# Where weight tiles begin within 128 bytes of SBUF in a two-layer decoder trunk

## The chip, the cores and the metric

One core of one Trainium2 chip runs the whole program in one launch. The metric is the device time of that launch in microseconds (us), lower is better. SBUF is the core's working memory: 128 partitions, and a tile is a run of bytes at the same address in every partition. Addresses below are bytes within a partition.

## What is computed

Two layers over 256 tokens of width 1024, all in float32, and a final norm (cut from the reference):

```
for l in range(2):
    hn = rms_norm(h, mix_norm_g[l])
    if l == 0: mix = even_mixer(hn, ...)   # softmax attention (8 heads x 64, rotary)
                                           # beside gated linear attention (8 heads), one output projection
    else:      mix = odd_mixer(hn, ...)    # gate branch x (width-4 conv -> RG-LRU recurrence), output projection
    h = h + mix
    h = h + conv_ffn(rms_norm(h, ffn_norm_g[l]), w_up, conv_w, conv_b, w_down)
return rms_norm(h, final_norm_g)

def conv_ffn(x, w_up, conv_w, conv_b, w_down):     # width 1024 -> 2 x 3072 -> 1024
    h = causal_dwconv(x @ w_up, conv_w, conv_b)    # width-3 depthwise convolution
    u, g = split(h, 2)
    return (u * gelu(g)) @ w_down
```

## The kernel before

Activations are kept with features on partitions and the 256 tokens along the row. All large weights are cut on the host into 204 chunks of 128 partitions x 1024 float32 (512 KB), in the order of use. A chunk is 8 blocks of 128 x 128.

A matmul with full float32 precision is made of three passes. Every operand is split in a high part (rounded to the format fp32r, which TensorE takes in one pass) and the low rest. `issue_w` (L123) fetches chunk i by a DMA of the SP queue into a landing tile `w`, makes the high part `wh` on ScalarE (L134) and the low part `wl` on VectorE (L135). `passes` (L142, matmuls at L146) then issues for each block three matmuls into one PSUM sum: wh times high activation, wh times low activation, wl times high activation. So a chunk makes 24 matmuls of 256 columns, each preceded on TensorE by a load of its 128 x 128 weights, and 204 chunks make 4,896 of them. In the listing of a trace wh, wh, wl follow each other. The split activations are the tiles `x` (input of a stage, L160 `new_x`), `m` and `r` (mixers' outputs) and `y` (FFN, 24 blocks); each of their rows of 256 float32 has 1,024 bytes. In one place, `tok_gemm` (PSUM tile `pst`, 8 chunks of layer 0), the roles are swapped: `x` is the loaded weight and `wh`/`wl` stream through.

The stages in order: layer 0 mixer (PSUM tiles psbq, psbk, psa, pst, psog and the attention pieces; `psout` is the output projection), layer 0 FFN (`psu` up, 96 chunks; `psd` down, 24 chunks), layer 1 mixer (psx, psgb, psgt, psout), layer 1 FFN (psu, psd), final norm. `Norm.rstd` (L181) turns summed squares into the norm's factor: two or four matmuls of one column into `nps` (L187), a square root and a reciprocal on `rtk`, and two transposes of `rtk` into `nps` (L193).

A scheduler fixes the order on each engine when the program is built, and an allocator gives each tile its address then; a tile's buffers are the distinct addresses that it gets. `issue_w` asks for 4 buffers of `w` and 6 of `wh` and `wl` (10 for the ten chunks from 104 on); the allocator may give more where there is room. `load_w` keeps one chunk issued ahead in the program; on the chip ScalarE, VectorE and the DMA queue run ahead as far as buffers allow.

In the built program the tiles that matter begin here (count of tiles by start address modulo 128 bytes):

```
tile                          before                 after
wh (204)                      189 at 96, 15 at 0     204 at 64
wl (204)                      180 at 96, 24 at 0     204 at 64
w, landing (204)              196 at 96, 8 at 0      204 at 0
x (4), m, r, y (FFN, 2)       all at 0               all at 0
chunks with wh and wl at 0    11                     0
chunks with only wl at 0      13                     0
chunks with only wh at 0      4                      0
```

Rows and blocks are multiples of 512 bytes, so every block of a tile has the tile's remainder. The chunks at 0 all lie in layer 1: numbers 106, 107, 124, 141, 147, 153, 159, 165, 171, 177 and 183 (both parts), 119, 123, 142, 148, 154, 160, 166, 172, 178, 184, 196, 197 and 198 (low part only), 118, 132, 186 and 200 (high part only). The landing tile's address comes round after 4 to 7 chunks in layer 0 and after 4 to 27 in layer 1 before (7 at the start of the kernel and in the layer 0 FFN), and after 4 chunks nearly everywhere after the change.

Of the kernel before, what the change touches and what calls it, by code (L numbers as in the profile page):

```python
# [8 lines left out]
F32 = mybir.dt.float32  # L9
F32R = mybir.dt.float32r  # L10
# [12 lines left out]
P = 128  # L23
S = 256
D = 1024
KT = 8
# [3 lines left out]
CW = 1024  # L30
# [18 lines left out]
NV = _o  # L49
# [13 lines left out]
def trunk(ctx: ExitStack, tc: tile.TileContext, xT, w, wgk, wgk2, vec, cst, mskf, out):  # L63
    nc = tc.nc

    cp = ctx.enter_context(tc.tile_pool(name="cp", bufs=1))
    wp = ctx.enter_context(tc.tile_pool(name="wp", bufs=4))
    xp = ctx.enter_context(tc.tile_pool(name="xp", bufs=1))
    tp = ctx.enter_context(tc.tile_pool(name="tp", bufs=2))
    pp = ctx.enter_context(tc.tile_pool(name="pp", bufs=1, space=bass.MemoryType.PSUM))  # L70

    def bank(name, tag="g"):
        return pp.tile([P, 512], F32, tag=tag, bufs=BANKS[tag], name=name)

    def order(first, then):
        tc.add_manual_dep(then.ins, first.ins.name,
                          mybir.DependencyInfo(mybir.DependencyClass.NoSync, mybir.DependencyReason.DATA),
                          reason="issue order")

    big = cp.tile([P, KT * S + P + NV + 8], F32, name="big")  # L80
    h = big[:, 0:KT * S].rearrange("p (k t) -> p k t", k=KT)
    idt = big[:, KT * S:KT * S + P]
    vt = big[:, KT * S + P:KT * S + P + NV]
# [22 lines left out]
    def act(name, *args, **kw):  # L106
        use(name)
        ins = nc.scalar.activation(*args, **kw)
        order(tbl["load"], ins)
        tbl["ops"].append(ins)  # L110
        return ins
# [6 lines left out]
    def load_w():  # L118
        while len(state["q"]) <= LOOK and state["i"] < NCH:
            state["q"].append(issue_w())  # L120
        return state["q"].pop(0)

    def issue_w():  # L123
        i = state["i"]
        state["i"] += 1
        wt = wp.tile([P, CW], F32, tag="w", name=f"w{i}")
        dma = nc.sync.dma_start(wt, w[i])
        if i == 0:
            first.append(dma)
        pre = "p" if L1_C0 <= i < L1_C0 + NPRE else ""  # L130
        nb = NPRE if pre else 6
        wh = wp.tile([P, CW], F32R, tag="wh" + pre, bufs=nb, name=f"wh{i}")
        wl = wp.tile([P, CW], F32R, tag="wl" + pre, bufs=nb, name=f"wl{i}")
        hi = nc.scalar.activation(wh, wt, AF.Copy)  # L134
        lo = nc.vector.tensor_sub(wl, wt, wh.bitcast(F32))  # L135
        for kind, o in (("h", hi), ("l", lo)):
            for before in state["hooks"].pop((kind, i), []):
                order(before, o)
        return wh, wl
# [24 lines left out]
    class Norm:  # L164
# [18 lines left out]
        def rstd(self, copy=True, hook=0):  # L183
            ps = bank("nps", "t")
            for t in range(2):
                for i, s_ in enumerate(self.acc):
                    nc.tensor.matmul(ps[:, t:t + 1], s_[:, t * P:(t + 1) * P], ones, start=i == 0,  # L187
                                     stop=i == len(self.acc) - 1)
            rt = tp.tile([P, 2], F32, tag="rtk", name="rtk")
            root = act(SQRT, rt, ps[:, 0:2], AF.Sqrt, bias=epst, scale=1.0 / D)  # L190
            inv = nc.vector.reciprocal(rt, rt)
            for t in range(2):
                nc.tensor.transpose(ps[:, S + t * P:S + (t + 1) * P], rt[:, t:t + 1].to_broadcast([P, P]), idt)  # L193
            self.tok = rt
            if not copy:
                return ps[:, S:2 * S]
            rs = tp.tile([P, S], F32, tag="rs", name="rs")
            cp_ = nc.scalar.activation(rs, ps[:, S:2 * S], AF.Copy)
            if hook:
                for key, o in zip((("h", hook), ("l", hook), ("h", hook + 1)), (root, inv, cp_)):  # L200
                    state["hooks"].setdefault(key, []).append(o)
            return rs
# [55 lines left out]
    for i in range(4):  # L258
        first.append(nc.sync.dma_start(h[:, 2 * i:2 * i + 2, :], xT[:, 2 * i:2 * i + 2, :]))
    state["q"].append(issue_w())  # L260
    first.append(nc.sync.dma_start(idt, cst[:, 0:P]))
    for a_, b_ in zip(first, first[1:]):
# [16 lines left out]
    with tc.tile_pool(name="l0", bufs=1) as lp, tc.tile_pool(name="l0r", bufs=4) as lr:  # L279
        def nt(name):  # L280
            return lr.tile([P, 512], F32, tag="n", bufs=14, name=name)

        state["q"].append(issue_w())
        state["q"].append(issue_w())
        gk2 = lp.tile([32, 256], F32, name="gk2")
# [82 lines left out]
        lam = vt[:, VOFF["lam"]:VOFF["lam"] + 8]  # L368

        def small(name):  # L370
            return cp.tile([P, 8], F32, name=name)

        e, d2, zz, z2, acc, cc = [small(f"s{i}") for i in range(6)]
        nc.scalar.activation(e, lam, AF.Abs)
        act(LNEXP, e, e, AF.Exp, scale=-1.0)
# [147 lines left out]
            return both  # L523

        def softmax(ps):
            mx = lr.tile([P, 2], F32, tag="mx", name="mx")
            nc.vector.tensor_reduce(mx[:, 0:1], ps[:, 0:128], axis=mybir.AxisListType.X, op=ALU.max)
            nc.vector.tensor_reduce(mx[:, 1:2], ps[:, 128:384], axis=mybir.AxisListType.X, op=ALU.max)
            nc.vector.tensor_scalar(mx, mx, -0.125, None, op0=ALU.mult)
            pe = lr.tile([P, 384], F32, tag="pe", name="pe")  # L530
            sm = lr.tile([P, 2], F32, tag="sm", name="sm")
            act(LNEXP, pe[:, 0:128], ps[:, 0:128], AF.Exp, bias=mx[:, 0:1], scale=0.125, accum_out=sm[:, 0:1])
            act(LNEXP, pe[:, 128:384], ps[:, 128:384], AF.Exp, bias=mx[:, 1:2], scale=0.125, accum_out=sm[:, 1:2])
            nc.vector.reciprocal(sm, sm)
            nc.vector.tensor_scalar(pe[:, 0:128], pe[:, 0:128], sm[:, 0:1], None, op0=ALU.mult)
            nc.vector.tensor_scalar(pe[:, 128:384], pe[:, 128:384], sm[:, 1:2], None, op0=ALU.mult)
            pt = bank("ptr", "t")
            for b in range(3):
                nc.tensor.transpose(pt[:, b * P:(b + 1) * P], pe[:, b * P:(b + 1) * P], idt)
            p_ = lr.tile([P, 384], F32, tag="PT", name="PT", bufs=8)  # L540
            nc.scalar.activation(p_, pt[:, 0:384], AF.Copy)
            return p_
# [3 lines left out]
        for pr in range(4):  # L546
            for j, ps in enumerate(scores(pr)):
                PT[2 * pr + j] = softmax(ps)
            ps = bank("pso", "t")
            for j in range(2):  # L550
                hd = 2 * pr + j
                r = slice(64 * j, 64 * j + 64)
                cs = slice(64 * hd, 64 * hd + 64)
                nc.tensor.matmul(ps[r, 0:S], av[:, 0, cs], PT[hd][:, 0:S], start=True, stop=False)
                nc.tensor.matmul(ps[r, P:S], av[:, 1, cs], PT[hd][:, S:384], start=False, stop=True)
            split(M[:, pr, 0, :], M[:, pr, 1, :], ps[:, :S])
# [26 lines left out]
            gemm(ps[:, :S], load_w(), X)  # L583
            nc.vector.tensor_mul(bog[:, m, :], ps[:, :S], rs)
        act(SILU, bog, bog, AF.Silu)
        rh = lp.tile([P, 16], F32, name="rh")
        act(SQRT, rh, psn[:, 0:16], AF.Sqrt, bias=epst, scale=1.0 / 64)
        nc.vector.reciprocal(rh, rh)
        rb = lp.tile([P, 16, 64], F32, name="rb")
# [268 lines left out]
```

## Time and profile before

| | |
|---|---|
| time, median of 3 runs | 637.37 us (637.22 to 638.85) |
| the profiled execution | 639.27 us, span of its instructions 637.5 us |
| PE (TensorE matmuls) busy | 622.5 us, 98% |
| PEld (weight loads, beside PE) | 608.1 us, 95% |
| DVE (VectorE) busy | 516.8 us, 81% |
| ACT (ScalarE) busy | 402.5 us, 63% |
| DMA | 110.91 MB, mean 174 GB/s |

The span runs from the first to the last instruction; 1.8 us of the profiled execution lie around it. Matmuls overlap each other in the trace: one lasts some 280 ns from its first read to its modelled end, but the next starts some 117 ns after it. So the distance between starts (called the step below) is what a matmul costs, and a busy PE says nothing of it. In a timeline, neighbouring instructions of one kind are merged: `x2` is two of them, and the row's first number is the start of the first.

### The profile page before, as it was taken

Reading aid. Unit: us, or ns where it says so; the run is one execution under the profiler, and the core shown is the slowest. Engines: PE = TensorE matmul, PEld = TensorE weight load, DVE = VectorE, ACT = ScalarE, POOL = GpSimd, SP = SyncE. Lnnn points to the kernel's source line nnn. Section 1 sums busy time; section 2 is a strip of 40 time slices with the busy share of each in tenths; the row PEclk is TensorE's granted clock in tenths of the full one; section 3 lists DMA queues with packets and bytes.
Section 4 is the critical chain, followed back from the end, with each engine's and each line's share of the span. In section 5 each row is a group of like instructions: output and inputs, shape, how many; then the busy total and the mean of one; then the engine's idle time right before and its main releaser. Section 6 shows DMA issues by size and latency. Waiting matters only on the chain.

```text
span 637.5 us, 12979 instructions
## 1 busy us (share of the span) xinstructions
PE 622.5 (98%) x5210; PEld 608.1 (95%) x5210; DVE 516.8 (81%) x899; ACT 402.5 (63%) x654; POOL 33.3 (5%) x58
## 2 busy tenths in 40 slices
PE   7989999999999999999999999999999999999995
PEld 3989988999999999999999999989999999999995
DVE  5799984677999999987688859996999999976532
ACT  7696565766666666665477488865676666674310
POOL 7480000000000000000000000000000000000000
PEclk9999999999999999999999999999999999999998
DMA  8624624324472585555568305554356465455201
GB/s 302 259 97 164 208 92 166 134 103 162 165 284 95 186 294 186 184 196 183 187 226 305 126 2 198 200 190 174 133 200 235 162 229 188 178 212 187 100 1 67
DMA packets 31517, 110.91 MB, mean 174 GB/s; under 512 B 3648, under 2 KB 4192, under 8 KB 31456
## 3 DMA queue, kind: packets, MB, share of 16 engines
q1 hardware_dynamic: 31456, 110.07, 48.4%
q8 instruction: 41, 0.67, 0.4%
q14 instruction: 20, 0.16, 0.1%
HBM read 109.01 MB, written 1.05 MB: 173 GB/s over the span
## 4 chain that ended last, share of the span: by engine, by line
PE 92%; DVE 3%; ACT 2%; issue 1%; DMA 1%; SPq 0%; DVEq 0%
PE psu L146 42%; PE psd L146 21%; PE psout L146 5%; PE pst L146 4%; PE psx L146 4%; PE psgb L146 3%; PE psa L146 2%; PE psog L146 2%; PE psgt L146 2%; DVE wl L135 1%; PE psbq L146 1%; PE pl L462 1%; PE psbk L146 1%; ACT wh L134 1%; DMA big<-xT 1%
## 5 line engine op out<-in xcount | busy, mean ns | idle before, releaser
L134 ACT ACTIVATE wh<-w 128x1024 fp32r<-128x1024 f32 x204 | 212.7, 1057 | 116.3 <-PE psu L146 71.8
L135 DVE TENSOR_TENSOR wl<-w,wh 128x1024 fp32r<-128x1024 f32 x204 | 248.3, 1226 | 41.0 <-ACT wh L134 39.9
L146 PE MATMUL psu<-x,wh 128*128 128x256 f32 x1536 | 270.5, 280 | 0.0
L146 PEld LDWEIGHTS psu<-x,wh 128*128 128x128 f32 x1536 | 234.4, 188 | 0.0
L146 PE MATMUL psu<-x,wl 128*128 128x256 f32 x768 | 214.1, 279 | 0.0
L146 PEld LDWEIGHTS psu<-x,wl 128*128 128x128 f32 x768 | 144.5, 188 | 0.0
L146 PE MATMUL psd<-y,wh 128*128 128x256 f32 x768 | 134.6, 279 | 0.0
L146 PEld LDWEIGHTS psd<-y,wh 128*128 128x128 f32 x768 | 117.0, 188 | 0.0
L146 PE MATMUL psd<-y,wl 128*128 128x256 f32 x384 | 106.6, 279 | 0.0
L644 DVE SCALAR_TENSOR_TENSOR c<-v,big,c 128x255 f32<-128x255 f32 (+1 forms) x192 | 84.4, 484 | 0.0
L146 PEld LDWEIGHTS psd<-y,wl 128*128 128x128 f32 x384 | 72.1, 188 | 0.0
L642 ACT ACTIVATE c<-v,big 128x256 f32<-128x256 f32 x96 | 51.7, 588 | 0.5 <-DVE v L637 0.5
L172 ACT ACTIVATE sq<-big 128x256 f32<-128x256 f32 x40 | 15.4, 407 | 50.8 <-DVE big L211 50.8
L211 DVE TENSOR_TENSOR big<-big,psd 128x256 f32<-128x256 f32 x16 | 6.7, 420 | 35.1 <-PE psd L146 35.1
L637 DVE TENSOR_TENSOR v<-psu,rs 128x512 f32<-128x512 f32 x48 | 33.0, 690 | 0.0
L146 PE MATMUL psout<-r,wh 128*128 128x256 f32 x128 | 23.1, 281 | 2.0 <-DVE r L729 2.0
L146 PE MATMUL pst<-wh,x 128*128 128x256 f32 x128 | 24.6, 288 | 0.0
L146 PE MATMUL psa<-x,wh 128*128 128x256 f32 x128 | 22.7, 280 | 1.8 <-DVE kn L394 1.8
L146 PE MATMUL psout<-m,wh 128*128 128x256 f32 x128 | 23.6, 286 | 0.0
L146 PE MATMUL psx<-x,wh 128*128 128x256 f32 x128 | 23.0, 281 | 0.0
L146 PE MATMUL psgb<-x,wh 128*128 128x256 f32 x128 | 22.7, 280 | 0.0
L99 ACT ACT_TABLE_LOAD x17 | 21.8, 1283 | 1.0 <-PEq L850 0.7
(200 smaller groups left out, 862.2 us busy)
## 6 DMA issues: line engine op xcount, KB each, us to landing
w<-w SPq DMA_DIRECT2D x204, 512.0 KB, 4.2
big<-xT SPq DMA_DIRECT2D x4, 256.0 KB, 4.9
out<-o SPq DMA_DIRECT2D x4, 256.0 KB, 2.4
ct<-cst SPq DMA_DIRECT2D x1, 384.0 KB, 7.6
big<-vec SPq DMA_DIRECT2D x1, 224.0 KB, 8.1
mf<-mskf SPq DMA_DIRECT2D x1, 192.0 KB, 5.0
wg<-wgk SPq DMA_DIRECT2D x1, 64.0 KB, 2.1
big<-cst SPq DMA_DIRECT2D x1, 64.0 KB, 7.2
```

Of the source, the lines that this page charges most:

```text
L99: ld = nc.scalar.preload_act_table_set(name)
L134: hi = nc.scalar.activation(wh, wt, AF.Copy)
L135: lo = nc.vector.tensor_sub(wl, wt, wh.bitcast(F32))
L146: out.append(nc.tensor.matmul(ps, a, b, start=first and i + j == 0, stop=last and i == n - 1 and j == 2, skip_group_check=skip))
L172: ins = nc.scalar.activation(sq, t, AF.Square)
L211: add = nc.vector.tensor_add(h[:, m, :], h[:, m, :], ps)
L462: nc.tensor.matmul(pv[:, :, :, cs], Kb[li, I][:, ts_], qv[:, :, :, cs], start=True, stop=True)
L637: nc.vector.tensor_mul(v, ps.rearrange("p (j t) -> p j t", j=2), rs[:, None, :].to_broadcast([P, 2, S]))
L642: nc.scalar.activation(c[:, j, :], v[:, j, :], AF.Identity, bias=V("fc_b", layer * 48 + ch), scale=wv(2))
L644: nc.vector.scalar_tensor_tensor(c[:, j, d:], v[:, j, 0:S - d], wv(2 - d), c[:, j, d:], op0=ALU.mult, op1=ALU.add)
```

## The change

The allocator packs tiles tightly, at multiples of 32 bytes. Tiles whose length is no multiple of 128 bytes are made longer until it is (`big`, `rtk`, the small tiles `s0` to `s5`, `mx`, `sm`, `rh`); `w`, `wh` and `wl` get 128 bytes more, and the used 4,096 bytes of `wh` and `wl` begin 64 bytes into them. What is computed stays as it was.

```diff
-    big = cp.tile([P, KT * S + P + NV + 8], F32, name="big")
+    big = cp.tile([P, -(-(KT * S + P + NV + 8) // 32) * 32], F32, name="big")
...
-        wt = wp.tile([P, CW], F32, tag="w", name=f"w{i}")
+        wt = wp.tile([P, CW + 32], F32, tag="w", name=f"w{i}")[:, 0:CW]
         dma = nc.sync.dma_start(wt, w[i])
...
-        wh = wp.tile([P, CW], F32R, tag="wh" + pre, bufs=nb, name=f"wh{i}")
-        wl = wp.tile([P, CW], F32R, tag="wl" + pre, bufs=nb, name=f"wl{i}")
+        oh, ol = 16, 16
+        wh = wp.tile([P, CW + 32], F32R, tag="wh" + pre, bufs=nb, name=f"wh{i}")[:, oh:oh + CW]
+        wl = wp.tile([P, CW + 32], F32R, tag="wl" + pre, bufs=nb, name=f"wl{i}")[:, ol:ol + CW]
...
-            rt = tp.tile([P, 2], F32, tag="rtk", name="rtk")
+            rt = tp.tile([P, 32], F32, tag="rtk", name="rtk")[:, 0:2]
...
-            mx = lr.tile([P, 2], F32, tag="mx", name="mx")
+            mx = lr.tile([P, 32], F32, tag="mx", name="mx")[:, 0:2]
```

The built program has the same instructions with other addresses, and lines from L132 on have moved by one. The order changes in the layer 0 mixer alone, in few places; the largest shift is around the first norm. On PE, in the second chunk of psbq and the first of psbk, before:

```order
L146 MATMUL psbq<-x,wh_158 128x256 x2
L146 MATMUL psbq<-x,wl_159 128x256
L146 MATMUL psbq<-x,wh_158 128x256 x2
L146 MATMUL psbq<-x,wl_159 128x256
L146 MATMUL psbk<-x,wl_165 128x256
L146 MATMUL psbk<-x,wh_164 128x256
L187 MATMUL nps<-big,ssq 128x1 x2
L146 MATMUL psbk<-x,wh_164 128x256
```

and after:

```order
L147 MATMUL psbq<-x,wl_159 128x256
L188 MATMUL nps<-big,ssq 128x1 x2
L147 MATMUL psbq<-x,wh_158 128x256 x2
L147 MATMUL psbq<-x,wl_159 128x256
L147 MATMUL psbq<-x,wh_158 128x256 x2
L147 MATMUL psbq<-x,wl_159 128x256
L147 MATMUL psbk<-x,wl_165 128x256
L147 MATMUL psbk<-x,wh_164 128x256 x2
```

The norm's sums now follow 44 of the chunk matmuls instead of 52, and its two transposes 73 instead of 87; the next step that needs the norm on PE, `psz` (L348), follows 96 in both. On VectorE, the conversions and the norm's sums of the same stretch, before:

```order
L135 TENSOR_TENSOR wl_165<-w_162,wh_164 128x1024
L179 TENSOR_TENSOR ssq<-ssq,sq 128x256
L135 TENSOR_TENSOR wl_373<-w_370,wh_372 128x1024
L179 TENSOR_TENSOR ssq<-ssq,sq 128x256
L135 TENSOR_TENSOR wl_403<-w_400,wh_402 128x1024
L135 TENSOR_TENSOR wl_446<-w_443,wh_445 128x1024
L191 RECIPROCAL rtk<-rtk 128x2
```

and after:

```order
L136 TENSOR_TENSOR wl_165<-w_162,wh_164 128x1024
L180 TENSOR_TENSOR ssq<-ssq,sq 128x256 x2
L136 TENSOR_TENSOR wl_373<-w_370,wh_372 128x1024
L136 TENSOR_TENSOR wl_403<-w_400,wh_402 128x1024
L192 RECIPROCAL rtk<-rtk 128x2
L136 TENSOR_TENSOR wl_446<-w_443,wh_445 128x1024
```

The last sum of squares and the reciprocal each moved ahead of one conversion. The SP and POOL queues keep their order.

## Rows read from the trace of the kernel before

**Rows 1.** The page: busy time of the engines, and the chain of work that ended last by engine.

```profile
PE 622.5 (98%) x5210; PEld 608.1 (95%) x5210; DVE 516.8 (81%) x899; ACT 402.5 (63%) x654; POOL 33.3 (5%) x58
...
PE 92%; DVE 3%; ACT 2%; issue 1%; DMA 1%; SPq 0%; DVEq 0%
```

**Rows 2.** What PE waited for over the whole span: us in total, times, longest.

```profile
PE psout L146 <- DVE r L729: 2.0, 2, 1.5
PE psa L146 <- DVE kn L394: 1.8, 1, 1.8
...
PE psbq L146 <- ACT wh L134: 0.9, 1, 0.9
...
PE psbq L146 <- DVE wl L135: 0.8, 1, 0.8
```

**Rows 3.** Busy time by stretch (layer 0 FFN up and down, layer 1 FFN up and down): us, PE busy (x instructions), PEld, DVE, ACT, POOL, granted clock, DMA share, GB/s.

```profile
155.00:275.00 120.00, 120.00 (x1031) 120.00 (x1030) 114.96 (x198) 81.42 (x133) 0.00 (x0) 1.00 0.55 196
275.00:343.00 68.00, 68.00 (x585) 68.00 (x585) 52.35 (x90) 41.27 (x56) 0.00 (x0) 1.00 0.58 205
...
440.00:560.00 120.00, 120.00 (x1023) 120.00 (x1022) 113.41 (x197) 80.50 (x131) 0.00 (x0) 1.00 0.54 193
560.00:628.00 68.00, 68.00 (x583) 68.00 (x582) 34.97 (x55) 26.08 (x36) 0.00 (x0) 1.00 0.31 109
```

**Rows 4.** Timeline of PE in the layer 0 FFN, wh and wl at 96: eight groups of wh, wh, wl lie between the first row and the last.

```profile
199.80 0.40 PE L146 MATMUL psu<-x,wh 128*128 128x256 f32 x2
200.03 0.28 PE L146 MATMUL psu<-x,wl 128*128 128x256 f32 x1
200.15 0.39 PE L146 MATMUL psu<-x,wh 128*128 128x256 f32 x2
...
202.60 0.40 PE L146 MATMUL psu<-x,wh 128*128 128x256 f32 x2
```

**Rows 5.** Timeline of PE in the layer 1 FFN: the first row begins chunk 153 (wh and wl at 0), the row at 487.57 chunk 154 (wl at 0), the last row chunk 155. Four groups of three lie between 486.01 and 487.45.

```profile
484.69 0.40 PE L146 MATMUL psu<-x,wh 128*128 128x256 f32 x2
...
486.01 0.28 PE L146 MATMUL psu<-x,wl 128*128 128x256 f32 x1
...
487.45 0.28 PE L146 MATMUL psu<-x,wl 128*128 128x256 f32 x1
487.57 0.40 PE L146 MATMUL psu<-x,wh 128*128 128x256 f32 x2
...
490.42 0.28 PE L146 MATMUL psu<-x,wh 128*128 128x256 f32 x1
```

**Rows 6.** Timeline of PE in `tok_gemm` of layer 0 (x at 0 loaded, wh and wl at 96 streaming): eleven groups of three lie between the first row and the last.

```profile
54.01 0.40 PE L146 MATMUL pst<-wh,x 128*128 128x256 f32 x2
...
57.91 0.40 PE L146 MATMUL pst<-wh,x 128*128 128x256 f32 x2
```

**Rows 7.** Groups of weight loads in two stretches, 479.1 to 481.7 (wh and wl at 96) and 484.7 to 487.4 (at 0): count, busy us, mean ns of one, idle before.

```profile
L146 PEld LDWEIGHTS psu<-x,wh 128*128 128x128 f32 x16 | 2.4, 188 | 0.0
...
L146 PEld LDWEIGHTS psu<-x,wh 128*128 128x128 f32 x16 | 2.5, 191 | 0.0
```

**Rows 8.** Timeline of the weight loads at the end, where the matmuls between them have one column.

```profile
629.58 0.30 PEld L187 LDWEIGHTS nps<-big,sq 128*128 128x128 f32 x2 [0.93 <-ACT sq L172]
629.80 0.30 PEld L187 LDWEIGHTS nps<-big,ssq 128*128 128x128 f32 x2
630.02 0.30 PEld L187 LDWEIGHTS nps<-big,sq 128*128 128x128 f32 x2
```

**Rows 9.** Timeline of the first 41 us, PE and then DVE: the norm's sums and transposes, psz, and the wait for `kn`.

```profile
20.16 0.50 PE L187 MATMUL nps<-big,ssq 128*128 128x1 f32 x4
...
24.69 0.38 PE L193 MATMUL nps<-big,rtk 128*128 128x128 f32 x2
...
26.28 1.13 PE L348 MATMUL psz<-bgk,gk 32*128 32x256 f32 x4
...
40.56 0.48 PE L146 MATMUL psa<-x,wh 128*128 128x256 f32 x2 [1.76 <-DVE kn L394]
...
16.51 1.31 DVE L135 TENSOR_TENSOR wl<-w,wh 128x1024 fp32r<-128x1024 f32 x1
17.74 0.72 DVE L179 TENSOR_TENSOR ssq<-ssq,sq 128x256 f32<-128x256 f32 x1
...
31.42 1.44 DVE L135 TENSOR_TENSOR wl<-w,wh 128x1024 fp32r<-128x1024 f32 x1 [0.34 <-ACT wh L134]
32.79 1.13 DVE L357 SCALAR_TENSOR_TENSOR G<-z,az 128x512 f32<-128x512 f32 x1
34.02 4.52 DVE L362 TENSOR_TENSOR_SCAN cum<-cum,G 128x512 f32<-128x512 f32 x3
38.47 1.35 DVE L135 TENSOR_TENSOR wl<-w,wh 128x1024 fp32r<-128x1024 f32 x1
39.74 0.68 DVE L394 TENSOR_TENSOR kn<-psbk,rs 128x512 f32<-128x512 f32 x1
```

**Rows 10.** The page's groups of the two conversions and its row of the chunk DMA (count, KB each, median us to landing); then from the timelines the low part of chunk 49 (DVE), the high part of chunk 53 (ACT) and the low part of chunk 53 (DVE), counted in the program's order.

```profile
L134 ACT ACTIVATE wh<-w 128x1024 fp32r<-128x1024 f32 x204 | 212.7, 1057 | 116.3 <-PE psu L146 71.8
L135 DVE TENSOR_TENSOR wl<-w,wh 128x1024 fp32r<-128x1024 f32 x204 | 248.3, 1226 | 41.0 <-ACT wh L134 39.9
...
w<-w SPq DMA_DIRECT2D x204, 512.0 KB, 4.2
...
177.62 1.25 DVE L135 TENSOR_TENSOR wl<-w,wh 128x1024 fp32r<-128x1024 f32 x1
...
186.23 1.06 ACT L134 ACTIVATE wh<-w 128x1024 fp32r<-128x1024 f32 x1 [0.45 <-PE psu L146]
...
187.85 1.25 DVE L135 TENSOR_TENSOR wl<-w,wh 128x1024 fp32r<-128x1024 f32 x1
```

More of the change, by code (lines that the diff above doesn't have):

```diff
@@ L370, in small @@
         def small(name):
-            return cp.tile([P, 8], F32, name=name)
+            return cp.tile([P, 32], F32, name=name)[:, 0:8]
         e, d2, zz, z2, acc, cc = [small(f"s{i}") for i in range(6)]
@@ L530, in softmax @@
             pe = lr.tile([P, 384], F32, tag="pe", name="pe")
-            sm = lr.tile([P, 2], F32, tag="sm", name="sm")
+            sm = lr.tile([P, 32], F32, tag="sm", name="sm")[:, 0:2]
             act(LNEXP, pe[:, 0:128], ps[:, 0:128], AF.Exp, bias=mx[:, 0:1], scale=0.125, accum_out=sm[:, 0:1])
@@ L585, in trunk @@
         act(SILU, bog, bog, AF.Silu)
-        rh = lp.tile([P, 16], F32, name="rh")
+        rh = lp.tile([P, 32], F32, name="rh")[:, 0:16]
         act(SQRT, rh, psn[:, 0:16], AF.Sqrt, bias=epst, scale=1.0 / 64)
```

## The prediction

> **What bounds the kernel now.** I read the page first. PE is busy for 98% of the span, and the chain of work that ended last runs through PE for 92% of it [rows 1]. A busy PE alone does not prove a bound, so I read next what PE waited for. The waits are few: 2.0 us for `r`, 1.8 us for `kn`, and under 1 us each for the first chunk's two conversions, the only time that PE waits for `wh` or `wl` at all [rows 2]. So DMA, ScalarE and VectorE deliver in time, and the time is the number of matmuls times the step between them. [...]
>
> The third view is the timeline of PE, for the step. In the layer 0 FFN 24 matmuls take 202.60 - 199.80 = 2.80 us, 116.67 ns each [rows 4]. The reader is to see that this is not the same everywhere. In chunk 153 twelve steps take 487.45 - 486.01 = 1.44 us, 120.0 ns each [rows 5]; the code, the shape and the stage's other work are those of its neighbours, but `wh` and `wl` begin at 0 modulo 128 bytes there and at 96 elsewhere. In `tok_gemm`, with the roles swapped, 33 steps take 57.91 - 54.01 = 3.90 us, 118.2 ns each [rows 6]. So the step depends on where the two operands lie. Taking the loaded operand's remainder minus the streamed one's, modulo 128: at 0 the step is 120.0, at 32 (0 - 96) 118.2, at 96 116.67. The loads show it too: 191 ns each at 0, 188 at 96 [rows 7].
>
> The change puts this difference at 64 in every chunk, `tok_gemm` included (0 - 64 is 64 too). No row shows 64. That is the one unknown that matters: there are 204 x 24 = 4,896 such matmuls, so one nanosecond of step is worth 4.9 us.
>
> **The change part by part.**
>
> *Chunks at 0 go away.* A chunk with both parts at 0 lasts 487.57 - 484.69 = 2.88 us, one with only `wl` at 0 490.42 - 487.57 = 2.85 us [rows 5], against 2.80 us [rows 4]. If the new place costs what 96 costs, the 11 chunks of the first kind give 11 x 0.08 = 0.88 us, the 13 of the second 13 x 0.05 = 0.65 us. The 4 with only `wh` at 0 are not among the rows; I take 0.05 as well, 0.2 us. Sum 1.7 us.
>
> *`tok_gemm`.* 8 x 24 = 192 steps from 118.2 to 116.67 give 0.3 us.
>
> *The other 168 chunks, 4,032 steps, go from 96 to 64.* The bounds from the nearest rows: above, the worst step seen, 120.0 ns, +3.33 x 4,032 = +13.4 us. Below, the loads' own pace: where the matmuls between have one column, a pair of loads starts 0.22 us after the pair before, 110 ns each [rows 8]. That is -6.67 ns a step. But VectorE is busy 114.96 and 113.41 of the 120.00 us of the up-projections [rows 3], which can therefore shrink by 5.0 and 6.6 us at most. The other 2,592 matmuls (4,896 less the 96 chunks of up-projection) would give 17.3 us; together about -29 us.
>
> Between these ends I take no change, 116.67 ns, for this reason. During a step the matmul reads 256 x 4 = 1,024 bytes of a partition and the next load 512. The matmul's reading place gains 512 bytes on the load's, four times 128, in every step, whatever the start; so the start can only decide whether one meeting more falls inside the step. That fits steps that differ by about one unit, 120.0 - 116.67 = 3.33 ns, and a value between for 32, where some steps would have the extra meeting and some not. Then the long steps fill one stretch of differences that holds 0 and ends near 32, and 96 is outside it. 64 lies between 32 and 96, outside as well. This is an inference from three points; a straight line from 32 to 96 would give 117.4 ns at 64, +3.1 us on the 4,032 steps. I count it in the rival below.
>
> *The first norm moves ahead* on PE by 8 matmuls (its sums) and 14 (its transposes), 0.9 and 1.6 us at 117 ns. Its sums start at 20.16 now [rows 9]; 0.9 us earlier the last sum of squares, which now also leads one conversion on VectorE, still stands before it: it ends at 18.46 now and about 1.2 us earlier then. The norm comes 1.6 us sooner, but `psz` keeps its place on PE (26.28), and the wait that follows, 1.76 us for `kn`, hangs on G, the scans and the conversion before `kn` on VectorE. G starts at 32.79, right behind a conversion (31.42, 1.44 us) that waited for its high part, and that one isn't touched. So the wait stays: 0 us, give or take 0.5.
>
> *Landing tiles come round after 4 chunks instead of up to 7.* The DMA of chunk k waits then for the low part of chunk k - 4. In the layer 0 FFN the low part of chunk 49 ends at 178.86 and the high part of 53 begins at 186.23 [rows 10]: 7.4 us, and a landing takes 4.2. The cover is 3.2 us there, and behind it the lead of a finished chunk before its use: chunk 53's low part ends at 189.1, and its matmuls are those of 200.1 on [rows 4, 10], 11 us later. Cost nothing. Without this cover a chunk would cost 4.2 + 1.06 + 1.23 = 6.5 us instead of 2.8.
>
> *Conversions and other tiles* at new addresses: VectorE and ScalarE have idle time in every stage, and nothing waits for them; the padding moves no extra byte. Nothing.
>
> Sum: -1.7 - 0.3 + 0 = -2.0 us. The profiled execution took 639.27 us (637.5 of span), 0.3% over the median; 2.0 us less is 637.3 by its own time, and **635.4 us** by the median of 637.37. A change within 0.3% (1.9 us) can't be told from none for this kernel, so the forecast itself lies on that line.
>
> **The rivals.**
>
> *The step falls further (27%).* 64 is as far from 0 as an address can be. If distance counts, one more unit goes: 113.33 ns, -3.33 x 4,896 = -16.3 us, with the 2.0 us 619.1; half a unit gives 627. For it: the step falls from 0 to 32 and to 96, which is 32 on the other side, and 110 shows room below. Against: 32 and 96, equally far from 0, differ by 1.5 ns, so distance alone isn't the measure. VectorE would still fit, 114.96 in 116.6 us, without room for more.
>
> *The step rises (18%), slower than before.* If 64 belongs to the long stretch with 0 and 32: 118.2 ns is +1.5 x 4,032 = +6.2 us; the chunks at 0 still gain about 0.8 and `tok_gemm` nothing: 643. At 120.0 it is +13.4 us, and +0.3 for each of the two others: 651. It decides from 0.5 ns on, where 4,032 steps eat the 2.0 us. For it: the value at 32 is nearer to 0's than to 96's. It would also come if the pattern repeated every 64 bytes; against that, 32 and 96 would be equal then, and they are not.
>
> *The address plays no part (4%)*, and chunk 153 is slow by what runs beside it: 637.4, no change. Against it stand the same chunks, every sixth one of the layer 1 FFN, and the neighbours at 116.67. [...]
>
> *Fewer landing tiles make PE wait (3%).* Each late chunk costs up to 3.7 us (6.5 - 2.8); two or three where the mixers and FFNs meet make 643 to 647. It decides where the lead of 11 us is gone.
>
> **How the numbers follow.** The forecast has 48%: 635.4, with a range of its own from 634.5 to 637. Its chance falls half on faster by over 0.3% and half within. Faster: 0.24 + 0.27 = 0.51. Same: 0.24 + 0.04 + a hundredth of the rise = 0.29. Slower: 0.17 + 0.03 = 0.20. The range goes from 619, a full unit less, to 645, past the 118.2 ns case; below it lie steps nearer 110 and above it those nearer 120, some 15 in 100 together.
>
> **What would show each step right or wrong.** In the timeline after, 24 matmuls of any FFN chunk in 2.80 us (116.67) with no chunk of 2.85 or 2.88; loads at 188 ns everywhere; 33 steps of `pst` in 3.85 us; 1,031 matmuls in 120 us of the layer 0 up-projection. 2.72 us a chunk is the first rival, 2.84 or more the second. The wait for `kn` near 1.8 us and no wait of PE for `wh` or `wl` past the first chunk show the other terms right. The prediction is wrong above all if 64 isn't like 96: the long stretch of differences may reach further than 32, or the units may not be what they seem.

## The result and the profile after

The changed kernel takes 627.63 us (median of 4 runs, 626.35 to 630.00) against 638.11 us for the kernel before on the same chip: a ratio of 0.984, with an interval of 0.982 to 0.986. That is 10.5 us, 1.6% less, where 2.0 us were forecast. The profiled execution took 628.50 us, its span is 626.7 us; before the span was 637.5 us.

The page and the waits of PE, the rows that answer to [rows 1, 2]:

```profile
PE 609.1 (97%) x5210; PEld 594.1 (95%) x5210; DVE 516.1 (82%) x899; ACT 404.2 (64%) x654; POOL 30.9 (5%) x58
...
PE 87%; DVE 4%; DMA 4%; ACT 3%; issue 2%; SPq 0%; DVEq 0%; ACTq 0%
```

```profile
PE psout L147 <- DVE r L730: 2.6, 2, 1.5
PE psx L147 <- ACT x L206: 2.3, 1, 2.3
PE psa L147 <- DVE kn L395: 1.8, 1, 1.8
```

PE is still the bound, but a wait of 2.3 us for `x` is new, and 4% of the chain now runs through DMA, where it was 1%.

The busy time by stretch of the FFN, as in [rows 3] (us, PE busy with its instructions, PEld, DVE, ACT, POOL, granted clock, DMA share, GB/s), up and down in layer 0, then in layer 1:

```profile
155.00:275.00 120.00, 120.00 (x1061) 120.00 (x1061) 117.63 (x206) 84.46 (x138) 0.00 (x0) 1.00 0.59 202
275.00:340.00 65.00, 65.00 (x576) 64.98 (x574) 46.93 (x80) 37.17 (x47) 0.00 (x0) 1.00 0.65 221
430.00:550.00 120.00, 120.00 (x1061) 120.00 (x1060) 114.51 (x199) 84.24 (x135) 0.00 (x0) 1.00 0.57 198
550.00:620.00 70.00, 68.79 (x607) 68.62 (x605) 37.59 (x59) 28.41 (x40) 0.00 (x0) 1.00 0.37 129
```

A window counts every matmul that lies in it in part, some 2.4 more than begin there: (1,061 - 2.4) x 113.3 ns are the 120 us. Before, 1,031 and 1,023 stood in windows of the same length. VectorE is now busy for 117.63 of 120 us, as close to a bound of its own as the forecast said for this step.

Timeline of PE over the chunk of layer 0 that begins at 197.33 (eight groups of wh, wh, wl between the first row and the last), and over eleven groups of `tok_gemm`:

```profile
197.33 0.39 PE L147 MATMUL psu<-x,wh 128*128 128x256 f32 x2
...
200.05 0.39 PE L147 MATMUL psu<-x,wh 128*128 128x256 f32 x2
```

```profile
51.35 0.40 PE L147 MATMUL pst<-wh,x 128*128 128x256 f32 x2
...
55.23 0.40 PE L147 MATMUL pst<-wh,x 128*128 128x256 f32 x2
```

24 matmuls take 2.72 us, 113.33 ns each, against 116.67 in [rows 4]. In the layer 1 FFN every chunk that nothing interrupts takes 2.72 us too: the chunks of 2.88 and 2.85 us of [rows 5] are gone. In `tok_gemm` the 33 steps of this piece take 3.88 us, 117.6 ns, hardly under the 118.2 of [rows 6]. Over all steps of its 8 chunks that follow each other without a gap the mean is 116.4, and it was 118.4 before.

Where the time went, by stage (us from the first matmul of a stage to the first of the next, read from the starts in the traces; the first line begins with the span, the last ends with the last chunk matmul):

```
stage                       before    after    difference
mixer of layer 0            140.68   139.34      -1.34
FFN of layer 0              202.27   196.71      -5.56
mixer of layer 1             81.98    84.92      +2.94
FFN of layer 1              203.42   196.60      -6.82
```

The two FFNs give 12.4 us. Each has 72 chunks, 48 up and 24 down (the 96 chunks of `psu` named above are those of both layers). The mixers have 1,440 of the 4,896 matmuls, whose steps alone would give 4.8 us at 3.33 ns each; instead the two mixers together are 1.6 us longer. The mixer of layer 1 lost most, and the place to look at is its start. PE, ScalarE and the clock there, after, and ScalarE at the same place before:

```profile
339.79 0.39 PE L147 MATMUL psx<-x,wh 128*128 128x256 f32 x2
342.48 0.39 PE L147 MATMUL psx<-x,wh 128*128 128x256 f32 x1 [2.30 <-ACT x L206]
```

```profile
338.58 1.07 ACT L135 ACTIVATE wh<-w 128x1024 fp32r<-128x1024 f32 x1 [0.34 <-DMA w<-w]
340.66 1.06 ACT L135 ACTIVATE wh<-w 128x1024 fp32r<-128x1024 f32 x1 [1.01 <-DMA w<-w]
341.62 0.40 ACT L173 ACTIVATE sq<-big 128x256 f32<-128x256 f32 x1
341.93 0.49 ACT L206 ACTIVATE x<-big 128x256 fp32r<-128x256 f32 x1
```

```profile
343.80:347.30 3.50, 3.50 (x19) 3.50 (x19) 2.77 (x3) 2.80 (x5) 0.00 (x0) 0.52 0.93 322
```

```profile
342.19 1.06 ACT L134 ACTIVATE wh<-w 128x1024 fp32r<-128x1024 f32 x1 [0.65 <-DMA w<-w]
343.60 0.42 ACT L172 ACTIVATE sq<-big 128x256 f32<-128x256 f32 x1 [0.34 <-DVE big L211]
343.92 0.49 ACT L205 ACTIVATE x<-big 128x256 fp32r<-128x256 f32 x1
```

The last block of `x` (L206) stands on ScalarE behind the high part of chunk 115, and this waits for its DMA. Before, that conversion began at 342.19, 0.8 us ahead of the stage's first matmul (342.94); after, at 340.66, 4.6 us behind it (336.05). So PE waits 2.30 us for `x`, and behind the wait the granted clock is 0.52 in the mean of 3.5 us, with 0.50 from 343.96 to 347.37: 19 matmuls lie in that stretch, which would hold 31 at 113.33 ns, and the steps there are 213 to 218 ns. An estimate of the whole: 2.3 us for `x`, some 1.7 us by the clock (half of the 3.4 us at 0.50), and 0.6 us more of waits for `r`. These 4.6 us are most of the 5.8 that separate +2.94 from what the steps alone would give in this stage (720 x 3.33 ns and 0.4 us for its chunks at 0).

### The profile page after: what moved, and what is told of

Same layout as the page of the kernel before. It is cut to its first block, busy times and chain, and to the rows that moved or that the text cites. A ratio compares the mean times of both kernels' runs of the same rounds, so it can differ in the third digit from the quotient of the medians.

```text
span 626.7 us, 13053 instructions
## 1 busy us (share of the span) xinstructions
PE 609.1 (97%) x5210; PEld 594.1 (95%) x5210; DVE 516.1 (82%) x899; ACT 404.2 (64%) x654; POOL 30.9 (5%) x58
## 4 chain that ended last, share of the span: by engine, by line
PE 87%; DVE 4%; DMA 4%; ACT 3%; issue 2%; SPq 0%; DVEq 0%; ACTq 0%
PE psu L147 42%; PE psd L147 17%; PE psout L147 6%; PE pst L147 4%; PE psgb L147 3%; DMA w<-w 3%; PE psx L147 3%; PE psog L147 2%; DVE wl L136 2%; PE psa L147 2%; PE psgt L147 2%; ACT wh L135 1%; PE psbq L147 1%; PE pl L463 1%; PE pss L520 1%
## 5 line engine op out<-in xcount | busy, mean ns | idle before, releaser
L135 ACT ACTIVATE wh<-w 128x1024 fp32r<-128x1024 f32 x204 | 214.3, 1060 | 141.9 <-PE psu L147 69.5
L136 DVE TENSOR_TENSOR wl<-w,wh 128x1024 fp32r<-128x1024 f32 x204 | 248.2, 1222 | 53.5 <-ACT wh L135 49.3
L147 PE MATMUL psu<-x,wh 128*128 128x256 f32 x1536 | 262.2, 276 | 0.0
L147 PEld LDWEIGHTS psu<-x,wh 128*128 128x128 f32 x1536 | 231.3, 188 | 0.0
L147 PE MATMUL psu<-x,wl 128*128 128x256 f32 x768 | 211.7, 276 | 0.0
L147 PE MATMUL psd<-y,wh 128*128 128x256 f32 x768 | 130.5, 276 | 0.0
L147 PEld LDWEIGHTS psd<-y,wh 128*128 128x128 f32 x768 | 115.5, 188 | 0.0
L147 PEld LDWEIGHTS psx<-x,wh 128*128 128x128 f32 x128 | 20.7, 199 | 2.5 <-ACT x L206 2.5
```

The source lines that it names most:

```text
L147: out.append(nc.tensor.matmul(ps, a, b, start=first and i + j == 0, stop=last and i == n - 1 and j == 2, skip_group_check=skip))
```

## The experiments

Three questions were open: whether the address alone makes the shorter step and by which rule; whether fewer landing tiles cause the wait for `x`; and whether a version without that wait is faster still. All steps below are read from starts in the traces. A table behind the runs puts them beside the addresses.

**Every start from 0 to 120.** One kernel with sixteen starts, eight bytes apart.

```diff
-        oh, ol = 16, 16
+        oh = ol = 2 * (i % 16)
```

> Chunk i has its two split weight tiles at 8 x (i modulo 16) bytes modulo 128 instead of all at 64; the streamed tiles stay at 0 and nothing else differs, so each of the sixteen starts has some six chunks in each up-projection. Known steps: 120.0 ns at 0, 118.3 at 32, 113.33 at 64, 116.67 at 96. Theory 'distance': the step falls step by step from 0 to a least value about 64 and rises again to 128, with values between the known ones at the starts between (some 116 at 48, some 115 at 80). Rival 'one place': 64 alone, within 8 bytes at most, gives 113.33, and all starts between 40 and 56 and between 72 and 120 stay at 116.67 or above. Rival 'blocks of 32 bytes': four flat pieces with jumps at multiples of 32. If some start gives under 113.33, 64 isn't the best one. Time by the first: near the kernel before, 635 to 641.

Measured: 647.71 us (one run; 635 to 641 was expected). There is no valley. Of nine whole chunks at 64 five come to 113.33 ns after a few steps; the four others stay at 117.7 to 119.1. The chunks of all fifteen other starts have means between 116.5 and 120.9 ns, but for one chunk at 88 that ran at 113.33. Those at 56 and 72 take 116.7 to 120.0, no nearer to 113 than those at 8 or 120. The theory "distance" falls, "blocks of 32 bytes" as well (72 isn't like 64), and "one place" stands. The values are also not single ones: chunks at 96 had 116.5 to 118.9.

**All at 96.**

```diff
-        oh, ol = 16, 16
+        oh, ol = 24, 24
```

> The changed kernel with the tiles at 96 instead of 64: same order, same landing tiles, same addresses but for these 32 bytes. Both theories: step 116.67 ns in all FFN chunks. They differ on the wait of 2.3 us for the norm's input x at the start of layer 1 and the half clock behind it (4.4 us together). Theory 'landing': four landing tiles instead of seven cost it at any step; the wait is here as well, and the time is 638.1 - 2.1 + 4.4 = 640. Rival 'the faster matmuls eat the lead': at 116.67 ns there is no wait, and the time is 636.

Measured: 649.01 us, a ratio of 1.016 (1.013 to 1.018). Both theories had the step wrong. The layer 0 window, at 96 after the change:

```profile
155.00:275.00 120.00, 120.00 (x1018) 120.00 (x1017) 113.69 (x195) 81.00 (x131) 0.00 (x0) 1.00 0.59 193
```

1,018 matmuls are 118.2 ns each, where the kernel before had 116.67 at 96. The remainder modulo 128 is the same, so it is not all that counts. The wait for `x` is here as well (2.1 us), at slower matmuls than before: "landing" held, "the faster matmuls eat the lead" fell.

**Weights at 0, streamed tiles at 64.**

```diff
-        oh, ol = 16, 16
+        oh, ol = 0, 0
-        return xp.tile([P, KT, 2, S], F32R, tag="x", name="x")
+        return xp.tile([P, KT * 2 * S + 32], F32R, tag="x", name="x")[:, 16:16 + KT * 2 * S].rearrange(...)
```

(`m`, `r` and `y` in the same way. The kernel has the start, here 16, in a variable; the arguments of `rearrange` are left out.)

> Split weights at 0 modulo 128, and the streamed tiles x, m, r and y moved to 64 instead. The tiles c1 of the layer 1 gates (96 matmuls) stay at 0. Theory 'difference': only the distance between the two operands counts; step 113.33 ns in the FFN chunks, 120.0 in the gate chunks, time as the changed kernel, 626 to 630. Rival 'the weights' own address': step 120.0 ns everywhere, 638.1 + 4,896 x 2.9 ns = 652.

Measured: 630.48 us, 0.987 (0.983 to 0.991); the window:

```profile
155.00:275.00 120.00, 120.00 (x1061) 120.00 (x1060) 117.64 (x204) 84.31 (x137) 0.00 (x0) 1.00 0.61 202
```

1,061 matmuls again, 113.33 ns. The gate chunks, whose streamed tile stayed at 0, run at 118.9 to 120.0 ns. So the difference between the two operands counts, not the weights' own place.

**All at 0.**

```diff
-        oh, ol = 16, 16
+        oh, ol = 0, 0
```

> The changed kernel with the weight tiles at 0 instead of 64, all else the same. Theory 'the address sets the step': 120.0 ns in every chunk and 638.1 + 4,896 x 2.9 ns = 652. Rival 'something else that the change did (order, landing tiles, room between tiles) made the steps shorter': 113.33 ns as in the changed kernel, 628.

Measured: 651.30 us, 1.019 (1.015 to 1.023), with most steps between 115 and 124 ns, 119.0 in the mean of the FFN chunks:

```profile
155.00:275.00 120.00, 120.00 (x1008) 120.00 (x1007) 111.09 (x189) 80.86 (x129) 0.00 (x0) 1.00 0.57 192
```

This kernel has the same instructions in the same order on every engine as the changed one, and every tile's room at the same address; 64 bytes of start make 21 to 24 us (651.30 less 630.01 and 627.63, the two medians of the changed kernel). Room, order and landing tiles have no part in the shorter step.

**The norm's input ahead of the conversions.** The last residual block of the layer 0 FFN and its `x` are put ahead of the conversions of chunks 112 and 113.

```diff
+            if gname == "mix_g" and m == KT - 1:
+                for key, o in zip((("l", L1_C0 + 8), ("h", L1_C0 + 9), ("l", L1_C0 + 9)), (add, hi, state["lo"])):
+                    state["hooks"].setdefault(key, []).append(o)
```

(`L1_C0` is 104. The lines that keep the two instructions of the split at hand are left out.)

> The changed kernel, with the last residual block of the layer 0 FFN, its norm input x and the low part of x ordered ahead of the conversions of chunks 112 and 113 on VectorE and ScalarE (after the change x stands behind the high part of chunk 115, which waits for its DMA). Theory 'landing': the matmuls' wait of 2.3 us for x and the half clock behind it (2.1 us) go away, 627.6 - 4.4 = 623. Rival 'the wait only moves': the conversions that are put back are late later, or the clock falls in another place, 626 to 628.

Measured: 629.79 us, 0.987 (0.985 to 0.988): nothing gained. The waits:

```profile
PE psout L147 <- DVE r L733: 2.8, 1, 2.8
PE psa L147 <- DVE kn L398: 2.6, 1, 2.6
PE psx L147 <- ACT x L206: 1.7, 1, 1.7
```

The edit did only part of what it should: the scheduler put the conversions of chunks 114 and 115 ahead of `x` and only that of 113 behind it, so `x` still waits for their DMA, 0.6 us less than before. And a single wait of 2.8 us for `r` at the end of the mixer takes the place of two of 1.1 and 1.5, with the granted clock at 0.57 in the mean from 409 to 413 us. What was gained at the start was lost at the end, as the rival said; that the wait for `x` goes away by order alone was not shown.

**More landing tiles, fewer pairs.**

```diff
-        wt = wp.tile([P, CW + 32], F32, tag="w", name=f"w{i}")[:, 0:CW]
+        wt = wp.tile([P, CW + 32], F32, tag="w", bufs=5, name=f"w{i}")[:, 0:CW]
-        nb = NPRE if pre else 6
+        nb = NPRE if pre else 5
```

> The changed kernel with five buffers of the landing tile asked for instead of four, and five pairs of split tiles instead of six to make room; the landing address now comes round after 5 to 11 chunks around the end of the layer 0 FFN, 5 in the up-projections. All weight tiles at 64. Theory 'landing': no wait for x at the start of layer 1, 623. Rival 'the faster matmuls eat the lead': the wait of some 2.3 us is still there, 627.6. If the sixth pair was needed, the matmuls wait for wh or wl, and it is slower than 628.

Measured: 627.20 us, 0.983 (0.980 to 0.986). Its waits:

```profile
PE psout L147 <- DVE r L730: 1.9, 2, 1.0
...
PE psa L147 <- DVE wl L136: 1.6, 1, 1.6
...
PE pst L147 <- DVE wl L136: 1.3, 1, 1.3
```

No wait for `x` is left, and the mixer of layer 1 takes 81.65 us instead of 84.92, with the granted clock at 1.00 in it. "Landing" held for the wait. The total is no better: 626.26 to 630.11 us. In the trace, the slowest of its four runs, PE waits 2.9 us for `wl` with the five pairs, and the mixer of layer 0 takes 142.85 us instead of 139.34. Not all of that is due to the pairs: the first chunk matmul begins 1.8 us later in this trace, and the granted clock is 0.50 for 6.8 us at the start, where the changed kernel's trace has 3.4 (12.87 to 16.28).

**The kernel before with longer streamed tiles.** Only room is added, nothing is shifted.

```diff
-        return xp.tile([P, KT, 2, S], F32R, tag="x", name="x")
+        return xp.tile([P, KT * 2 * S + 32], F32R, tag="x", name="x")[:, 0:KT * 2 * S].rearrange(...)
```

(`m`, `r` and `y` in the same way.)

> The kernel before with the tiles x, m, r and y made 128 bytes longer and nothing else: weight tiles stay 4,096 bytes apart and at 96 modulo 128 (some 22 chunks of layer 1 at 0), but modulo 512 they now begin 224 behind the streamed tiles, 480 before; and the landing address comes round after 4 chunks. Theory 'landing': the wait for x at the start of layer 1 appears here too, some 2 us and 2 of half clock, 642. Rival: no wait, 638. For the step: if only the remainder modulo 128 counts, 116.67 ns in the layer 0 FFN as before; if more of the address counts, 116.65 to 117.75, as in the chunks at 224 of the run at 96.

Measured: 644.69 us, 1.010 (1.008 to 1.011). Up-projection, a piece of the down-projection, and the wait:

```profile
155.00:275.00 120.00, 120.00 (x1031) 120.00 (x1030) 114.96 (x199) 81.79 (x133) 0.00 (x0) 1.00 0.59 198
290.00:330.00 40.00, 40.00 (x339) 40.00 (x338) 28.10 (x55) 20.84 (x29) 0.00 (x0) 1.00 0.59 195
```

```profile
PE psx L147 <- ACT x L206: 1.5, 1, 1.5
```

With the landing tiles at 4 the wait is there at the old pace, and the mixer of layer 1 takes 85.58 us, 3.6 more than before, with the clock at 1.00 throughout; 1.5 us of them are this wait, and what the others are was not taken apart. The up-projection has its 1,031 matmuls as before, but the down-projection takes 118.8 ns a step, 40 us by 339 - 2.4. The weights lie 96 behind its streamed tile `y` modulo 128 in both kernels, but modulo 256 it is 96 here and 224 before; for `x` it is 224 in both.

**Four bytes to either side, and one part alone.**

```diff
-        oh, ol = 16, 16
+        oh, ol = ((16, 16), (15, 15), (16, 16), (17, 17), (16, 16), (16, 0), (16, 16), (0, 16))[i % 8]
```

> The changed kernel with other starts in every other chunk: chunks 8n have both parts at 64, 8n + 1 at 60, 8n + 3 at 68, 8n + 5 the high part at 64 and the low part at 0, 8n + 7 the reverse, all others at 64. Theory 'one place': 60 and 68 lose what 64 gives and run at 117 to 119 ns; a chunk with one part at 64 lies between, and the even chunks come back to 113.33 after a few steps. Rival 'a valley': 60 and 68 give 113.33 or one cycle more. Time 631 by the first, 628 by the second.

Measured: 640.12 us (one run; 631 by the first theory). Chunks at 60 run at 117.8 to 119.5 ns, chunks at 68 at 117.8 to 119.0, so four bytes are enough to lose all of it. With one part at 64 and one at 0 the chunks take 115.5 to 118.7, a few 120.0. What was not expected: of the 70 chunks with both parts at 64, 39 run at 113.33 and 31 at 117.7 to 119.1 to their end, none between. So 64 has two paces. Here the chunks between them lie at other starts, so what runs ahead of a chunk is a likely cause of its pace; no run shows the rule.

**Six pairs held for layer 1, landing after 4 and after 7 chunks.** Two kernels. Both hold six pairs instead of ten; the first, the control, asks for `bufs=4`, which is what the changed kernel has, and the second for 7:

```diff
-NPRE = 10
+NPRE = 6
-        wt = wp.tile([P, CW + 32], F32, tag="w", name=f"w{i}")[:, 0:CW]
+        wt = wp.tile([P, CW + 32], F32, tag="w", bufs=7, name=f"w{i}")[:, 0:CW]
```

> The changed kernel with six split pairs held for the start of layer 1 instead of ten, landing address still round after 4 chunks; the control of the next run. Theory 'landing': the wait for x at the start of layer 1 is still there, 1 to 3 us, and the time within 2 us of the changed kernel, 626 to 629. Rival 'the ten pairs made the burst': with six of them fewer conversions stand before x and the wait is gone, 623.

> As the run before, with the landing address round after 7 chunks through layer 0, as in the kernel before the change; all weight tiles at 64. Theory 'landing': no wait for x at the start of layer 1 and no half clock behind it, 4 us under its control, 622 to 624; conversions of the FFN stages wait less for their DMA. Rival 'the faster matmuls eat the lead': the wait is as in its control, 626 to 629.

Measured: 635.09 us (0.995, 0.993 to 0.998) after 4 chunks, where 626 to 629 was expected, and 628.01 us (0.983, 0.981 to 0.985) after 7, where 622 to 624 was. First some waits of the control, then all of PE's waits above 1.4 us in the second kernel:

```profile
PE psout L147 <- DVE r L728: 2.9, 1, 2.9
PE psa L147 <- DVE kn L395: 2.5, 1, 2.5
PE psout L147 <- DVE r L730: 2.3, 1, 2.3
...
PE psx L147 <- ACT x L206: 1.3, 1, 1.3
```

```profile
PE psout L147 <- DVE r L730: 2.8, 1, 2.8
PE psout L147 <- DVE r L728: 2.4, 1, 2.4
```

With seven landing tiles the wait for `x` is gone at the full pace of 113.33 ns. In the eleven traces with the address round after 4 chunks (all but three) the high part of chunk 115 begins 2.5 to 4.7 us behind the stage's first matmul, and PE waits 0.2 to 2.7 us for `x`; in the three others (before, five and seven tiles) it begins between 0.8 ahead and 0.1 behind, and `psx` has no such wait.

The mixer of layer 1 takes 84.57 us all the same, against 86.61 in the control. PE waits 5.2 us for `r` in both, twice the 2.6 of the changed kernel, and in both the granted clock is 0.50 for 6.8 us there (405.4 to 412.3 with seven tiles). So this longer wait is not what the seven tiles brought; the six pairs are what the two kernels share, and why `r` is waited for longer with them is not shown. The control's times, 631.7 to 639.1 us over 12 runs, go with the granted clock that was noted for each run: the six up to 634.7 us have means of 0.984 to 0.990, the six from 635.5 us on 0.977 to 0.982. Its trace is of the fastest run, so the two medians, 7.1 us apart, can't be put down to the wait for `x`, which is worth 2.0 us of the mixer in the traces.

**Streamed tiles at 32, weights at 96.**

```diff
-        return xp.tile([P, KT * 2 * S + 32], F32R, tag="x", name="x")[:, 0:KT * 2 * S].rearrange(...)
+        return xp.tile([P, KT * 2 * S + 32], F32R, tag="x", name="x")[:, 8:8 + KT * 2 * S].rearrange(...)
```

(Against the kernel before with longer streamed tiles; `m`, `r` and `y` in the same way.)

> The kernel of the run with longer streamed tiles, where the weight tiles lie at 96 modulo 128 (22 of each in layer 1 at 0), with x, m, r and y begun at 32. Nothing lies at 64 now, but the difference is 64 for the chunks at 96 and 96 for those at 0. Theory 'difference': 113.33 ns in the whole layer 0 FFN, 117 to 119 in the chunks at 0 and in some chunk behind each; 644.7 - 14 = 630. Rival 'one of the two operands must begin at 64': steps of 117 to 120 everywhere, 640 to 648.

Measured: 639.04 us (1.000, 0.998 to 1.003; 635.0 to 642.5 over 10 runs), where 630 was expected. The two up-projections and the end of the last down-projection:

```profile
155.00:275.00 120.00, 120.00 (x1022) 120.00 (x1021) 114.05 (x195) 81.00 (x131) 0.00 (x0) 1.00 0.60 194
...
455.00:575.00 120.00, 120.00 (x1022) 120.00 (x1021) 112.99 (x199) 80.80 (x132) 0.00 (x0) 1.00 0.57 190
```

```profile
586.00:630.00 44.00, 44.00 (x391) 44.00 (x390) 19.37 (x27) 13.22 (x16) 0.00 (x0) 1.00 0.33 108
```

The last row is 113.3 ns a step, with no operand at 64: the short step doesn't need one there, and the rival falls. But the difference of 64 isn't enough for it. The whole FFN of layer 0 runs at 117.7 ns with the same difference in every chunk. Of its 129 chunks at a difference of 64, 24 run at 113.33 and 105 at 117.7 or 117.8. The ten times don't go with the granted clock of their runs (641.4 us at 0.997, 635.0 at 0.996), so the pace may differ from run to run; one trace can't show it.

**The changed kernel again.**

> The changed kernel again, for a second trace and more times. At a difference of 64 the traces show two paces, 113.33 ns and some 117.75 ns; behind an interruption of the row of matmuls one of them sets in and can last for hundreds of matmuls. Theory 'the program decides': both up-projections run at 113.33 as in the first trace, and all times lie within 626 to 631. Rival 'chance decides': a stage of this trace is at 117.75 from its start on, or some times lie 5 us or more above the others (576 matmuls of a down-projection at the slow pace cost 2.5 us, 1,152 of an up-projection 5.1).

Measured: 630.01 us, 0.987 (0.985 to 0.989), 629.2 to 630.5. The window and the wait:

```profile
155.00:275.00 120.00, 120.00 (x1061) 120.00 (x1060) 117.67 (x204) 84.65 (x138) 0.00 (x0) 1.00 0.61 202
```

```profile
PE psx L147 <- ACT x L206: 2.1, 1, 2.1
```

The FFNs take 196.65 and 196.60 us, as in the first trace (196.71 and 196.60). Of the chunks that nothing interrupts, 120 runs at the slow pace to its end in both traces, 9 in the second alone. So in the FFNs two traces of this kernel give the same paces, as they would if the order of the program decides; two traces don't rule out chance. The clock, though, fell elsewhere this time: behind the wait for `kn` in layer 0 (2.2 us; 0.65 in the mean from 41 to 44 us), not behind that for `x` (1.00 from 343.8 to 347.3): the mixer of layer 0 took 141.34 us and that of layer 1 83.61.

The chunks that nothing interrupts, of six traces (before, changed, at 96, at 0, streamed at 64, longer streamed tiles) by the two differences modulo 256, ns a step behind the first eight of a chunk:

```
wh - streamed, wl - streamed     chunks   mean
0, 0                                 29   119.98
128, 128                             43   119.60
0, 128                               51   119.11
128, 0                               43   118.43
96, 96                               62   118.60
224, 96                              43   118.65
96, 224                              50   117.87
224, 224                            244   116.78
64 or 192, each                     288   113.33 in 276, 117.8 to 119.1 in 12
```

(15 chunks of the kernels before and with longer streamed tiles, with one part 224 or 128 behind and the other at 0, 96 or 128, are left out.) Modulo 256 the rows are single or close; modulo 128 they were not: 96 and 224 fall together there, with 118.6 and 116.8.

## Why the prediction was wrong

**What bounds the kernel** was read rightly: PE's step, which depends on where the two operands lie. Moving every weight tile by 64 bytes, with nothing else changed, made 21 to 24 us. With the granted clock at 1.00 the step is 113.33 to 120.0 ns by where PE's own two operands begin. That meetings of their two reads decide it was the author's inference; no run shows why the places matter.

**The step that failed** is the term "the other 168 chunks go from 96 to 64", sized at nothing: it was 116.67 - 113.33 = 3.33 ns, -13.4 us over 4,032 steps. Two inferences stood under it. The first was that the difference modulo 128 sets the step. It does not: the chunks of the kernel before that stood for "96" were all 224 apart modulo 256, and at 96 modulo 256 the step is 118.6, so that one of the three points was not what it was taken for. The second was that a long stretch of differences behaves alike and 64 lies outside it with 96. There is no such stretch: of the eighteen starts tried, 64 alone gives 113.33 to more than a single chunk. The row that the working did not have was any at 64, and the text said so; sizing it by its neighbours was the mistake, when no row showed that neighbours are alike. Equal chances for the three steps that fit the units (113.33, 116.67, 120.0) would have been the better reading. That the kernel became faster, as forecast, is mostly owed to this term: the two terms that the forecast was made of came to 2.0 us.

**The first rival**, that the step falls a full unit, was right on the step: 113.33 ns in every FFN chunk that nothing interrupts. Its 619.1 us was 8.5 too low. By the profiled spans its 18.3 us became 10.8. The FFNs paid nearly in full: 5.56 us of 1,728 x 3.33 = 5.8 in layer 0, and 6.82 of 5.8 + 1.3 for the chunks at 0 in layer 1 (8 x 0.08, 14 x 0.05). What is missing, 7.5 us, lies nearly all in the mixers: 5.8 in that of layer 1 and 1.4 in that of layer 0.

**"Landing tiles come round after 4 chunks: cost nothing"** was the other step that failed. Its cover was read in the layer 0 FFN, where it holds: PE waits for no `wh` or `wl` there. It was not read where many conversions come at once, at the end of that FFN, where ten pairs of split tiles are free to be filled and ScalarE works off chunks 104 to 115 as they land; the one that is late there is not a chunk but `x`, queued behind them. The price was 2.3 us of wait and 3.4 us at a granted clock of 0.50; at the old pace, with longer streamed tiles and so four landing tiles, the mixer of layer 1 lost 3.6 us, 1.5 of them this wait. The rival on landing tiles, at 3%, came true together with the first one.

**The rest held.** The norm's earlier place on PE changed nothing: the wait for `kn` is 1.8 us in the first trace of both kernels. The chunks at 0 are level with the others. `tok_gemm` fell about as far as said over all its chunks, from 118.4 to 116.4 ns, but by little, to 117.6, in the piece that was to show it. The conversions cost what they did (1,060 and 1,222 ns against 1,057 and 1,226). The loads' own time was no sign of the step: it is 188 ns at 113.33 as it was at 116.67.

```profile
L147 PEld LDWEIGHTS psu<-x,wh 128*128 128x128 f32 x1536 | 231.3, 188 | 0.0
```

What stays open: why 64, and why modulo 256 for the rest; what chooses between the two paces at 64; why `r` is waited for longer with six held pairs; and how fast the kernel would be with seven landing tiles, six pairs in layer 0, ten held pairs and a shorter chain to `r`. No version tried beats the changed kernel beyond its interval.

## What to carry to other kernels

Where PE is the bound, read the step from start to start, per chunk, and put it beside the start addresses of both operands: a few bytes of alignment between the loaded and the streamed tile were worth 12.4 us of 638 in the two FFNs here, and a price at an address that no row shows is unknown, not that of its neighbour. A faster PE comes sooner to every wait that was hidden: before counting steps times nanoseconds, list what arrives just in time in the stages with dependencies (here `x` behind queued conversions, 2.3 us, and `r`, 2.6 us against 2.0 before), since 7.5 of 18.3 us did not arrive, 5.8 of them in the mixer of layer 1. Padding that moves tiles also changes how many buffers an allocator finds (here of the landing tiles, from 7 to 4 in the layer 0 FFN); look for the place where the most transfers come at once, not at the steady stage.

## What the runs showed of the hardware that was not expected

- Two paces at one address. At a difference of 64 a row of matmuls runs either at 113.33 ns (113, 113, 114) or at 117.75 (117, 118, 118, 119), nothing between over a chunk, and keeps its pace for long (1,640 matmuls in the changed kernel, from 154.0 to 339.9 us). It changed behind interruptions (one-column matmuls, transposes, waits) and behind chunks at another difference. In the FFNs of the changed kernel the fast pace sets in within some 20 steps each time, but chunk 120 of its layer 1 mixer stays at 117.8 to its end; with streamed tiles at 32 the slow one stayed through the whole FFN of layer 0.
- The place is sharp: 60 and 68 run at 117.8 to 119.5 ns.
- A row of the kernel before (224 modulo 256) has one mean, 116.67, in two patterns of steps: 116, 117, 117 in layer 0, and 113, 116, 117, 120 behind the chunks at 0 in layer 1.
- The granted clock fell to 0.50 behind waits of PE between 2.1 and 2.8 us (for `x` in the changed kernel, for `kn` in its second trace, for `r` with seven landing tiles, where two waits of 2.4 and 2.8 us nearly meet), and stayed there for 3.4 us, or 6.8 in the last. It did not fall behind every such wait: the second trace has 2.1 us for `x`, and the kernel with the norm's input ahead 2.6 us for `kn`, with the clock at 1.00 behind them. By the estimate above, the wait for `x` in the changed kernel cost nearly twice what the list of waits shows (2.3 us and some 1.7). The twelve times of the control with six pairs, 7.4 us apart, go with the mean granted clock of their runs, 0.990 to 0.977.
